# Output projection of a state-space layer divided at half of its 2048 channels, with the decay differences of two head groups on ScalarE

## The chip, the cores and the metric

The kernel runs on one core of one Trainium2 chip. The metric is the device time of one execution in microseconds. A core has five engines that work through instruction streams of their own, each in order: PE (TensorE, with its weight loads shown as PEld), DVE (VectorE), ACT (ScalarE), POOL (GpSimd) and SP (SyncE, which here only issues DMAs). They wait for one another by semaphores.

## The reference

Two layers run over two streams, a prompt of 256 tokens and a sample of 64 with carried state; the kernel treats them as 320 columns side by side. Layer one is a Mamba-2 mixer and a convolutional feed-forward block, layer two is latent attention (MLA) and another such block. Only the Mamba-2 mixer is touched. Cut to what matters:

```
zxbcdt = h @ w_in                                   # 1024 -> 2048 z, 3072 x/B/C, 32 dt
xbc_c  = silu(causal_dwconv(xbc, ...))
dtp    = softplus(dt + dt_bias);  a = -exp(a_log)
# per chunk: acs = cumsum(dtp * a)
seg    = acs[:, :, :, None] - acs[:, :, None]
decay  = exp(where(causal, seg, -inf))
y_diag = einsum(cb * decay * dtp, x);  states, y_off from exp(acs_end - acs), exp(acs)
yg     = rmsnorm over each of 4 groups of 512 channels of (y * silu(z))
out    = yg @ w_out                                 # 2048 -> 1024
```

There are 32 heads of 64 channels in 4 groups of 8 heads; a group is 512 of the 2048 channels.

## The kernel before, in words

**Precision and weights.** Everything is fp32. A product is made of three matmuls (`mm3`, L283 twice and L284 once): high half of the weights by high half of the values, high by low, low by high. Weights come as tiles of 128x1024 fp32 (512 KB) through a ring: SP issues the DMA of a tile into one of 3 buffers `wr`, ACT copies out the high half `wh` (L326), DVE subtracts to get the low half `wl` (L328); there are 4 buffers of each half. Tiles are fetched up to 5 ahead of the one in use (`LD`) and split up to 3 ahead (`LS`).

**Order.** The program is written as a sequence of steps; a scheduler with a simulated timeline then sets the order of the instructions on each engine, by what it reckons is ready. So an edit in one place can move instructions in another. The table `PLAN` sets the sequence in the state-space layer by group g: `conv` (input projection and convolution of x, B, C), `z` (input projection of the gate), `fetch`, `decay`, `scan`, `gate`. The third number says how many pending small steps are let in after each block.

**Decay.** `ssd_fetch` brings, for each of three chunks of 128, 128 and 64 positions, the cumulated log decays of 8 heads, broadcast over the partitions, into a tile `dc` of n x 8 x n elements. `diff` then makes own minus `dc` on DVE (L876, all eight heads in one instruction; L874 first copies out the last column), and clamps it at zero on ACT (L877). `ssd_decay` takes the exponentials on ACT.

**Scan.** `ssd_steps` has 13 small steps per group: `pre` (B and C products, L906 and L907), `xpose` (L918, with `xa` written by DVE L925), `diag` (L935, the products within a chunk, and L943, with the carried state), `states` (L952) and `skip` (L967).

**Gate.** `gate_steps` has three: multiply by silu(z) and square (L982 to L985), sum over the tokens on PE (L362) and the inverse root by Newton steps on DVE (L344 to L350), then `spread` on PE (L369), the multiplication by it on DVE (L992) and the split of each 128-channel block into `ah` (ACT L329) and `al` (DVE L330).

**Output projection.** The 2048 channels are 16 blocks kb of 128 (4 per group), the 1024 outputs 8 blocks m of 128. A product of one block by one output is three matmuls of 320 columns, so the projection has 384. It is divided at channel block 12. The first part takes blocks 0 to 11 (groups 0 to 2) for outputs 0 to 3 and then 4 to 7, in `square_part`: four PSUM tiles `pm` held at once, six weight tiles per half, and after each weight tile `step()` puts in two of the scan and gate steps that are still pending (`LAST` = 2). ACT copies the results into `y` (L771), except that output 7 stays in its PSUM tile. The second part takes blocks 12 to 15 (group 3) for one output after the other; `post` adds the first part (L487, DVE), squares and scales (L497 and L498, ACT) and adds the square to `yacc` (L500, DVE). Before block 15 of output 7, `post_seven` sums `yacc` over the tokens (L362) for the norm that follows.

**Other lines.** L649 and L647 are the convolution, L640 the copy into its input `ext`, L668 the silu, L735 the copy of a gate block out of PSUM, L757 the save of the convolution rows at the end, L644 the POOL copy that feeds it.

Of the kernel before, what the change touches and what calls it, by code (L numbers as in the profile page):

```python
# [17 lines left out]
T = 320  # L18
# [14 lines left out]
DCB = 2  # L33
OUT = 6, 7
SEVEN = 15
# [50 lines left out]
class Kern:  # L86
# [590 lines left out]
    def ssm(self):  # L677
# [3 lines left out]
        with ExitStack() as st:  # L681
# [5 lines left out]
            with ExitStack() as s2:  # L687
# [79 lines left out]
                for half in range(2):  # L767
                    ps = [self.pm() for _ in range(4)]
                    self.square_part(ah, al, range(0, 12, 2), ps, step, 4 - half)
                    for n in range(4 - half):  # L770
                        nc.scalar.activation(out=self.y[:, 4 * half + n, :], in_=ps[n][:, :T], func=AF.Copy)  # L771
                while late:
                    step()
            for half in range(2):
                w = [self.nextw(), self.nextw()]
                for n in range(4):
                    m = 4 * half + n
                    if m > 3:
                        self.early_step(early)
                    p = ps[3] if m == 7 else self.px()  # L780
                    for kb in range(12, 16):
                        if m == 7 and kb == SEVEN:
                            self.post_seven()
                            end = self.pe_end
                        wh, wl = w[kb // 2 - 6]
                        q = slice((kb % 2 * 4 + n) * 128, (kb % 2 * 4 + n) * 128 + 128)
                        last = self.mm3(p[:, :T], wh[:, q], wl[:, q], ah[:, kb, :], al[:, kb, :], kb == 12 and m < 7, kb == 15,
                                        end if m == 7 else None)
                    end = last
                    self.post(p, m, "mix_post0", m < 7)  # L790
# [62 lines left out]
    def ssd_fetch(self, g, sp):  # L853
# [15 lines left out]
        def diff(c):  # L869
            n = CHUNKS[c][1]  # L870
            dc = self.dc[g][c]
            q = 32 * c + 8 * g
            if c:
                nc.vector.tensor_copy(out=self.cd[:, c, 8 * g:8 * g + 8].unsqueeze(2), in_=dc[:, :, n - 1:n])  # L874
            own = self.dtt[:n, 192 + q:200 + q].unsqueeze(2).to_broadcast([n, 8, n])
# [3 lines left out]
        return load, [lambda c=c: diff(c) for c in range(3)]  # L879
# [524 lines left out]
def layout(i):  # L1404
# [16 lines left out]
    wo = f["ssm_w_out"][0].reshape(8, 2, 128, 2, 4, 128).transpose(3, 0, 2, 1, 4, 5).reshape(2, 8, 128, 1024)  # L1421
    out["w_out"] = np.ascontiguousarray(np.concatenate([wo[0, :6], wo[1, :6], wo[0, 6:], wo[1, 6:]], 0))
# [92 lines left out]
```

## Time and profile before

| | |
|---|---|
| median of three timed runs | 995.41 us (995.04 to 996.72) |
| the profiled execution, its own time | 998.17 us |
| its span, first to last instruction | 996.4 us |
| granted TensorE clock over the span | 0.985 |
| 0 to 60 us | PE busy 51.66 us, clock 0.97 |
| 60 to 196.1 us (state-space layer up to the output projection) | PE busy 134.56 of 136.10 us, clock 1.00 |
| 196.1 to 275 us (output projection and its end) | PE busy 75.63 of 78.90 us, clock 0.95 |
| 275 to 996.4 us (the rest of the program) | PE busy 698.07 of 721.40 us, clock 0.99 |

The rows of the trace that follow later give, for a group of instructions, the source line, engine, operation, `out<-in` with the names of the program and shapes, then count, busy time and mean duration; in square brackets stands how long the engine was idle just before and what released it. Rows of a window give its length, then busy time and count for PE, PEld, DVE, ACT and POOL, the granted clock as a share of full speed, the busy share of the DMA engines and GB/s.

### The profile page before, as it was taken

The page shows a single profiled execution, that of the slowest core. Times are in us where ns is not written, and L with a number is a line of the kernel's source. Part 1 is how long each engine was busy: PE and PEld are TensorE (multiplying, and loading weights), DVE is VectorE, ACT ScalarE, POOL GpSimd, SP SyncE. Part 2 cuts the span into 40 slices and gives each one's busy share as a digit, 9 for nine tenths or more (in the row PEclk, how much of TensorE's full clock was granted, in tenths as well). Part 3 has the DMA queues.
Part 4 walks back from the last instruction along what each step waited for, and adds up shares of the span by engine and source line. Part 5 has one row for each costly group of instructions (what it writes and reads, how often), then busy time and mean ns, then how long its engine had stood idle before and what let it go on. Part 6 is the DMA issues. An engine that isn't in the chain of part 4 may idle for free.

```text
span 996.4 us, 18044 instructions
## 1 busy us (share of the span) xinstructions
PE 959.9 (96%) x6585; PEld 929.7 (93%) x6585; DVE 757.7 (76%) x1437; ACT 605.1 (61%) x1201; POOL 350.7 (35%) x597
## 2 busy tenths in 40 slices
PE   7899999999999999999999999999999999999995
PEld 6899999979989999999999899999999999999994
DVE  7879889797488998774547998886538999775433
ACT  6568886734556687664443677774544778665330
POOL 4823231200045665430005765530004767441001
PEclk9999999998999999999999999999999999999998
DMA  7376646442334544455641222133443455445531
GB/s 251 120 212 190 188 138 204 132 154 96 101 94 131 169 149 150 149 186 165 194 125 35 86 70 78 50 102 114 143 136 105 132 167 169 150 143 145 152 115 54
DMA packets 45802, 135.55 MB, mean 136 GB/s; under 512 B 5392, under 2 KB 9616, under 8 KB 45712
## 3 DMA queue, kind: packets, MB, share of 16 engines
q1 hardware_dynamic: 45424, 134.05, 43.1%
q8 instruction: 52, 0.85, 0.4%
q14 instruction: 38, 0.31, 0.1%
q10 hardware_dynamic: 288, 0.33, 0.1%
HBM read 130.25 MB, written 4.11 MB: 135 GB/s over the span
## 4 chain that ended last, share of the span: by engine, by line
PE 79%; DVE 10%; DMA 3%; POOL 3%; issue 3%; ACT 2%; SPq 0%; POOLq 0%; ACTq 0%; DVEq 0%
PE pm L283 46%; PE pm L284 23%; PE px L283 2%; DMA dc<-acd 2%; PE pr L362 1%; PE px L952 1%; DVE wl L328 1%; POOL xacc L442 1%; PE px L284 1%; PE px L943 1%; PE px L935 1%; ACT wh L326 1%; DVE mx L1267 1%; POOL xn L478 1%; DVE y L450 1%
## 5 line engine op out<-in xcount | busy, mean ns | idle before, releaser
L328 DVE TENSOR_TENSOR wl<-wr,wh 128x1024 fp32r<-128x1024 f32 (+2 forms) x204 | 244.8, 1201 | 115.4 <-ACT wh L326 114.6
L326 ACT ACTIVATE wh<-wr 128x1024 fp32r<-128x1024 f32 (+4 forms) x235 | 227.6, 972 | 154.2 <-PE pm L283 126.7
L283 PE MATMUL pm<-xnh,wh 128*128 128x320 f32 x784 | 243.4, 312 | 2.1 <-ACT xnh L329 1.8
L283 PE MATMUL pm<-xnl,wh 128*128 128x320 f32 x784 | 245.0, 313 | 0.3 <-DVE xnl L330 0.3
L284 PE MATMUL pm<-xnh,wl 128*128 128x320 f32 x784 | 243.1, 311 | 0.0
L283 PEld LDWEIGHTS pm<-xnh,wh 128*128 128x128 f32 x784 | 147.6, 189 | 4.8 <-ACT xnh L329 2.0
L283 PEld LDWEIGHTS pm<-xnl,wh 128*128 128x128 f32 x784 | 147.8, 189 | 1.7 <-issue 1.2
L284 PEld LDWEIGHTS pm<-xnh,wl 128*128 128x128 f32 x784 | 147.8, 189 | 1.2 <-issue 1.2
L284 PE MATMUL pm<-ah,wl 128*128 128x320 f32 x452 | 141.0, 313 | 0.0
L283 PE MATMUL pm<-al,wh 128*128 128x320 f32 x452 | 140.4, 311 | 0.0
L283 PE MATMUL pm<-ah,wh 128*128 128x320 f32 x452 | 139.9, 313 | 0.0
L649 DVE SCALAR_TENSOR_TENSOR cv<-ext,vec,cv 128x322 f32<-128x322 f32 x176 | 97.1, 566 | 5.4 <-ACT cv L647 3.0
L643 POOL COPY fsave<-ext 128x2 f32<-128x2 f32 x88 | 72.2, 821 | 53.4 <-ACT ext L640 49.1
L636 POOL MEMSET ext<- 128x2 f32 (+1 forms) x112 | 10.8, 98 | 221.3 <-DVE al L330 66.0
L283 PEld LDWEIGHTS pm<-ah,wh 128*128 128x128 f32 x452 | 85.3, 190 | 1.7 <-ACT ah L329 1.5
L284 PEld LDWEIGHTS pm<-ah,wl 128*128 128x128 f32 x452 | 85.4, 189 | 1.1 <-issue 1.0
L283 PEld LDWEIGHTS pm<-al,wh 128*128 128x128 f32 x452 | 85.5, 189 | 0.0
L328 POOL TENSOR_TENSOR wl<-wr,wh 128x512 fp32r<-128x512 f32 (+2 forms) x31 | 43.7, 1425 | 102.3 <-ACT wh L326 100.9
L283 PE MATMUL pm<-xgl,wh 128*128 128x320 f32 x220 | 68.4, 314 | 1.0 <-DVE xgl L426 1.0
L284 PE MATMUL pm<-xgh,wl 128*128 128x320 f32 x220 | 68.3, 314 | 1.0 <-DVE wl L330 0.7
L283 PE MATMUL pm<-xgh,wh 128*128 128x320 f32 x220 | 62.6, 316 | 4.6 <-ACT xnh L329 2.4
L647 ACT ACTIVATE cv<-ext,vec 128x322 f32<-128x322 f32 x88 | 57.0, 654 | 10.0 <-POOL ext L637 6.8
(396 smaller groups left out, 2138.5 us busy)
## 6 DMA issues: line engine op xcount, KB each, us to landing
wr<-w_up SPq DMA_DIRECT2D x76, 512.0 KB, 3.3
wr<-w_in SPq DMA_DIRECT2D x37, 512.0 KB, 3.8
wr<-w_dn SPq DMA_DIRECT2D x32, 512.0 KB, 3.5
wr<-w_out SPq DMA_DIRECT2D x16, 512.0 KB, 3.6
wr<-w_o SPq DMA_DIRECT2D x16, 512.0 KB, 3.4
wr<-w_up_k SPq DMA_DIRECT2D x16, 384.0 KB, 3.1
wr<-w_dn SPq DMA_DIRECT2D x16, 384.0 KB, 3.2
dc<-acd SPq DMA_DIRECT2D x8, 512.0 KB, 7.0
```

The source lines that it names most:

```text
L283: for i in (mm(out, wh, xh, start=first, stop=False), mm(out, wh, xl, start=False, stop=False), mm(out, wl, xh, start=False, stop=last)):
L284: mm(out, wl, xh, start=False, stop=last)):
L326: self.high_ins = nc.scalar.activation(out=hdst, in_=src, func=AF.Copy).ins
L328: return lambda: e.tensor_tensor(out=ldst, in0=src, in1=hdst.bitcast(F32), op=ALU.subtract)
L362: i = self.nc.tensor.matmul(ps[:, o + b:o + b + 1], acc[:, l0:l0 + 128], self.ones[:, 0:1], start=True, stop=True)
L442: nc.gpsimd.tensor_tensor(out=acc, in0=acc, in1=s, op=ALU.add)
L450: tt(out=yk, in0=yk, in1=r, op=ALU.mult)
L478: nc.gpsimd.tensor_tensor(out=xn, in0=self.x[:, k, :], in1=rstd, op=ALU.mult)
L636: nc.gpsimd.memset(ext[:, 0:m], 0.0)
L643: nc.gpsimd.tensor_copy(out=rows_out[:, 0, :], in_=ext[:, TP:TP + m])
L647: nc.scalar.activation(out=c, in_=ext[:, 0:n], func=AF.Identity, scale=w(0), bias=b)
L649: nc.vector.scalar_tensor_tensor(out=c, in0=ext[:, i:i + n], scalar=w(i), in1=c, op0=ALU.mult, op1=ALU.add)
```

## The change

The projection is divided at channel block 8 in place of 12. The first part now takes groups 0 and 1 only, with four weight tiles per half. The second part takes groups 2 and 3. Its weights are laid out anew on the host, so that one tile of 128x1024 holds blocks 8 to 15 of one output. Outputs 0, 1 and 2 are taken together: group 2's blocks for all three, held in three PSUM tiles `px` with their three weight tiles, then group 3's blocks for all three. Outputs 3 to 7 follow one by one, each with its eight blocks and one weight tile.

For groups 2 and 3 (`WIDE` = 2) `diff` no longer makes one DVE subtraction and one ACT clamp per chunk. ACT does both in one instruction per head: clamp at zero of (−1 · `dc` + own), where own is a column with one value per partition, the bias. It is cut into two pieces of four heads. The copy of the last column stays on DVE. Groups 0 and 1 are as they were.

Lines move by 1 up to the state-space layer's function and by 9 from the scan on (L283 becomes L284, L369 becomes L370, L935 becomes L944); the new ACT instruction is L881.

```
--- before.py
+++ after.py
@@ -31,6 +31,7 @@
         ('z', 3, 3), ('silu', 3, 0), ('gate', 3, 0))
 LAST = 2
 DCB = 2
+WIDE = 2
 OUT = 6, 7
 SEVEN = 15
 LEAD = 2
@@ -766,28 +767,31 @@
 
                 for half in range(2):
                     ps = [self.pm() for _ in range(4)]
-                    self.square_part(ah, al, range(0, 12, 2), ps, step, 4 - half)
+                    self.square_part(ah, al, range(0, 8, 2), ps, step, 4 - half)
                     for n in range(4 - half):
                         nc.scalar.activation(out=self.y[:, 4 * half + n, :], in_=ps[n][:, :T], func=AF.Copy)
                 while late:
                     step()
-            for half in range(2):
-                w = [self.nextw(), self.nextw()]
-                for n in range(4):
-                    m = 4 * half + n
+            for ms in ((0, 1, 2), (3,), (4,), (5,), (6,), (7,)):
+                w, p = {}, {}
+                for m in ms:
                     if m > 3:
                         self.early_step(early)
-                    p = ps[3] if m == 7 else self.px()
-                    for kb in range(12, 16):
-                        if m == 7 and kb == SEVEN:
-                            self.post_seven()
-                            end = self.pe_end
-                        wh, wl = w[kb // 2 - 6]
-                        q = slice((kb % 2 * 4 + n) * 128, (kb % 2 * 4 + n) * 128 + 128)
-                        last = self.mm3(p[:, :T], wh[:, q], wl[:, q], ah[:, kb, :], al[:, kb, :], kb == 12 and m < 7, kb == 15,
-                                        end if m == 7 else None)
-                    end = last
-                    self.post(p, m, "mix_post0", m < 7)
+                    w[m] = self.nextw()
+                    p[m] = ps[3] if m == 7 else self.px()
+                for ks in (range(8, 12), range(12, 16)):
+                    for m in ms:
+                        wh, wl = w[m]
+                        for kb in ks:
+                            if m == 7 and kb == SEVEN:
+                                self.post_seven()
+                                end = self.pe_end
+                            q = slice((kb - 8) * 128, (kb - 8) * 128 + 128)
+                            last = self.mm3(p[m][:, :T], wh[:, q], wl[:, q], ah[:, kb, :], al[:, kb, :], kb == 8 and m < 7, kb == 15,
+                                            end if m == 7 else None)
+                        end = last
+                        if kb == 15:
+                            self.post(p[m], m, "mix_post0", m < 7)
 
     def ssm_conv(self, i, ps, rstd, sp):
         g, i = divmod(i, 10)
@@ -866,17 +870,22 @@
                     for p, r in ((slice(0, 64), r0), (slice(64, 128), r0 + 4)):
                         self.issue(nc.sync.dma_start(out=ea[p].rearrange("p h l -> p (h l)"), in_=src(r, r + 4, 64)))
 
-        def diff(c):
+        def diff(c, hs):
             n = CHUNKS[c][1]
             dc = self.dc[g][c]
-            q = 32 * c + 8 * g
-            if c:
+            q = 192 + 32 * c + 8 * g
+            if c and 0 in hs:
                 nc.vector.tensor_copy(out=self.cd[:, c, 8 * g:8 * g + 8].unsqueeze(2), in_=dc[:, :, n - 1:n])
-            own = self.dtt[:n, 192 + q:200 + q].unsqueeze(2).to_broadcast([n, 8, n])
+            if len(hs) < 8:
+                for h in hs:
+                    nc.scalar.activation(out=dc[:n, h, :], in_=dc[:n, h, :], func=AF.Relu, scale=-1.0, bias=self.dtt[:n, q + h:q + h + 1])
+                return
+            own = self.dtt[:n, q:q + 8].unsqueeze(2).to_broadcast([n, 8, n])
             nc.vector.tensor_tensor(out=dc[:n], in0=own, in1=dc[:n], op=ALU.subtract)
             nc.scalar.activation(out=dc[:n], in_=dc[:n], func=AF.Relu)
 
-        return load, [lambda c=c: diff(c) for c in range(3)]
+        m = 8 if g < WIDE else 4
+        return load, [lambda c=c, h=h: diff(c, range(h, h + m)) for c in range(3) for h in range(0, 8, m)]
 
     def ssd_decay(self, g):
 
@@ -1418,8 +1427,10 @@
             cols += [z[:, g * 512:g * 512 + 512]]
     w = np.concatenate(cols, 1)
     out["w_in_k"], out["w_in"] = _outer(w, 4), _blocks(w[:, 512:])
-    wo = f["ssm_w_out"][0].reshape(8, 2, 128, 2, 4, 128).transpose(3, 0, 2, 1, 4, 5).reshape(2, 8, 128, 1024)
-    out["w_out"] = np.ascontiguousarray(np.concatenate([wo[0, :6], wo[1, :6], wo[0, 6:], wo[1, 6:]], 0))
+    wo = f["ssm_w_out"][0].reshape(2, 1024, 1024)
+    first = wo[0].reshape(4, 2, 128, 2, 4, 128).transpose(3, 0, 2, 1, 4, 5).reshape(8, 128, 1024)
+    rest = wo[1].reshape(8, 128, 8, 128).transpose(2, 1, 0, 3).reshape(8, 128, 1024)
+    out["w_out"] = np.ascontiguousarray(np.concatenate([first, rest], 0))
     out["w_o"] = _square(f["mla_w_o"][0])
     for l in range(2):
         u = f["ffn_w_up"][l].reshape(D, 2, NBF, 128)
```

The scheduler's orders differ between group 1's scan and the end of this projection, and nowhere else. Three places follow; in the names, the numbers behind an underscore tell buffers apart.

**First place: PE, the last scan steps of group 3**, before. L362 and L369 here belong to the gate of group 2.

```order
L362 MATMUL pr_2357<-ones_73,sz_2135 128x1 x3
L935 MATMUL px_2535<-dc_359_2125,xa_2531 64x128 x8
L943 MATMUL px_2544<-ct_1847,hp_2475 128x128 x4
L952 MATMUL px_2551<-xa_2532,bcs_2428 128x512
L918 MATMUL px_2603<-con_71,xs_1911 64x128
L918 MATMUL px_2603<-con_71,xs_1971 64x128
L918 MATMUL px_2603<-con_71,xs_2029 64x128
L918 MATMUL px_2603<-con_71,xs_2089 64x128
L369 MATMUL pr_2373<-con_71,rk_2363 128x128 x3
L935 MATMUL px_2612<-dc_361_2130,xa_2608 64x64 x8
L943 MATMUL px_2621<-ct_1847,h_387_2318 128x64 x4
L952 MATMUL px_2658<-xa_2609,bcs_2490 128x512
```

And in the changed kernel:

```order
L284 MATMUL pm_2608<-ah_101,wh_2611 128x320
L284 MATMUL pm_2608<-al_102,wh_2611 128x320
L285 MATMUL pm_2608<-ah_101,wl_2612 128x320
L944 MATMUL px_2648<-dc_361_2148,xa_2644 64x64 x8
L952 MATMUL px_2657<-ct_1865,h_387_2354 128x64 x4
L961 MATMUL px_2694<-xa_2645,bcs_2526 128x512
L284 MATMUL pm_2804<-ah_101,wh_2666 128x320
L284 MATMUL pm_2804<-al_102,wh_2666 128x320
L285 MATMUL pm_2804<-ah_101,wl_2667 128x320
```

Before, the last two chunks' `diag` and `states` of group 3 stood one behind the other. Now only the last chunk's three lines stand together, with matmuls of the projection's first part (`pm`, values `ah`) ahead of them and behind them.

**Second place: ACT, where the differences of group 2 are made**, before (`dc`, the tile of the decays; `hp`, the carried state; `sz`, the gate):

```order
L326 ACTIVATE wh_1600<-wr_1462 128x1024
L326 ACTIVATE wh_1640<-wr_1520 128x1024
L735 ACTIVATE sz_1597<-pm_1604 128x320
L668 ACTIVATE ct_1306<-ct_1306 128x323
L640 ACTIVATE ext_1494<-pm_1468 128x256
L640 ACTIVATE ext_1494<-pm_1468 128x64
L877 ACTIVATE dc_274_1585<-dc_274_1585 128x1024
L647 ACTIVATE xs_1493<-ext_1494,vec_70 128x323
L955 ACTIVATE hp_1330<-px_1328 128x512
```

And in the changed kernel:

```order
L327 ACTIVATE wh_1600<-wr_1462 128x1024
L881 ACTIVATE dc_274_1585<-dc_274_1585,dtt_613 128x128 x8
L327 ACTIVATE wh_1640<-wr_1520 128x1024
L736 ACTIVATE sz_1597<-pm_1604 128x320
L669 ACTIVATE ct_1306<-ct_1306 128x323
L641 ACTIVATE ext_1494<-pm_1468 128x256
L641 ACTIVATE ext_1494<-pm_1468 128x64
L648 ACTIVATE xs_1493<-ext_1494,vec_70 128x323
L881 ACTIVATE dc_275_1587<-dc_275_1587,dtt_613 128x128 x4
L964 ACTIVATE hp_1330<-px_1328 128x512
L881 ACTIVATE dc_275_1587<-dc_275_1587,dtt_613 128x128 x4
L327 ACTIVATE wh_1676<-wr_1598 128x1024
```

One L877 per chunk is replaced by eight L881, in pieces of four or eight between weight splits (L327) and the instructions of the convolution.

**Third place: PE, the spread of group 3's gate (L369, now L370)**, before, among matmuls of the first part (`pm`):

```order
L283 MATMUL pm_2831<-ah_101,wh_2766 128x320
L283 MATMUL pm_2831<-al_102,wh_2766 128x320
L284 MATMUL pm_2831<-ah_101,wl_2767 128x320
L369 MATMUL pr_2751<-con_71,rk_2711 128x128 x3
L283 MATMUL pm_2829<-ah_101,wh_2796 128x320
L283 MATMUL pm_2829<-al_102,wh_2796 128x320
```

And in the changed kernel, among matmuls of group 2 for the outputs 0 to 2 (`px_2939` is output 0, `px_2946` output 1):

```order
L284 MATMUL px_2946<-ah_101,wh_2870 128x320
L284 MATMUL px_2946<-al_102,wh_2870 128x320
L285 MATMUL px_2946<-ah_101,wl_2871 128x320
L284 MATMUL px_2946<-ah_101,wh_2870 128x320
L370 MATMUL pr_2787<-con_71,rk_2747 128x128 x3
L284 MATMUL px_2946<-al_102,wh_2870 128x320
L285 MATMUL px_2946<-ah_101,wl_2871 128x320
L284 MATMUL px_2946<-ah_101,wh_2870 128x320
```

Before, 91 matmuls of the first part stood between it and the first matmul on group 3's halves. Now it stands behind 19 of the 36 matmuls of group 2 for outputs 0 to 2, and 17 stand between it and the first matmul on group 3's halves.

## The prediction

> **What bounds the kernel now.** I read the share of each engine first, then a table of windows around the output projection, the waits of PE in it, and last the timeline where the table shows a loss.
>
> ```profile
> PE 959.9 (96%) x6585; PEld 929.7 (93%) x6585; DVE 757.7 (76%) x1437; ACT 605.1 (61%) x1201; POOL 350.7 (35%) x597
> ```
>
> PE is the bound, 96% of the span. Moving work between DVE and ACT pays only where PE stands or runs slowly. The next view has per window: length, busy time (and count) of PE, PEld, DVE, ACT, POOL, the granted clock, DMA share and GB/s.
>
> ```profile
> 113.60:140.00 26.40, 26.40 (x194) 24.53 (x193) 25.42 (x45) 18.16 (x33) 11.02 (x16) 1.00 0.54 159
> 150.00:196.10 46.10, 46.10 (x338) 42.85 (x336) 41.06 (x75) 30.70 (x53) 9.89 (x10) 1.00 0.54 170
> 196.10:211.40 15.30, 15.30 (x104) 14.81 (x104) 14.99 (x24) 10.24 (x15) 0.00 (x0) 1.00 0.47 163
> 211.40:229.80 18.40, 16.04 (x110) 12.09 (x109) 18.10 (x41) 3.88 (x8) 0.24 (x2) 0.81 0.32 105
> 255.50:273.00 17.50, 16.59 (x114) 16.10 (x113) 9.20 (x17) 11.65 (x23) 0.00 (x0) 1.00 0.31 91
> ```
>
> The first three are PE without a gap at full clock. From 211.4 to 229.8 PE has gaps, the clock is 0.81, and DVE is busy 18.10 of 18.40 us. PE's waits from 140 to 275 us, all of them:
>
> ```profile
> PE px L935 <- DVE xa L925: 1.2, 1, 1.2
> PE px L935 <- issue: 1.1, 1, 1.1
> PE pr L362 <- ACT ysq L493: 0.5, 1, 0.5
> PE pr L362 <- DVE yacc L500: 0.4, 1, 0.4
> ```
>
> The first two lie in that window, the last two at the end of the projection (near 271 us). The timeline shows why (start, duration):
>
> ```profile
> 216.08 1.09 PE L935 MATMUL px<-dc,xa 128*64 128x128 f32 x16 [1.07 <-issue]
> 221.50 0.68 PE L935 MATMUL px<-dc,xa 64*64 64x64 f32 x16 [1.24 <-DVE xa L925]
> 222.12 1.64 PE L943 MATMUL px<-ct,h 128*128 128x64 f32 x8
> 223.69 2.07 PE L952 MATMUL px<-xa,bcs 64*128 64x512 f32 x2
> 225.69 1.44 PE L283 MATMUL pm<-ah,wh 128*128 128x320 f32 x4
> 227.19 0.47 PE L284 MATMUL pm<-ah,wl 128*128 128x320 f32 x1
> 227.46 0.47 PE L283 MATMUL pm<-al,wh 128*128 128x320 f32 x1
> 230.07 0.31 PE L283 MATMUL pm<-al,wh 128*128 128x320 f32 x1
> 230.22 0.31 PE L284 MATMUL pm<-ah,wl 128*128 128x320 f32 x1
> ```
>
> Two projection matmuls start 0.15 us apart at 230 us, 0.27 us apart at 227 us. Between 211.8 and 225.7 PE has hardly any projection work, because the next block row is group 2, whose halves come from ACT L329. The three rows below are groups 1, 2 and 3; DVE L992 releases group 2 only at 223.47.
>
> ```profile
> 199.67 1.91 ACT L329 ACTIVATE ah<-yg,vec 128x320 fp32r<-128x320 f32 x4
> 223.47 1.92 ACT L329 ACTIVATE ah<-yg,vec 128x320 fp32r<-128x320 f32 x4 [9.59 <-DVE yg L992]
> 244.97 1.93 ACT L329 ACTIVATE ah<-yg,vec 128x320 fp32r<-128x320 f32 x4 [0.94 <-DVE yg L992]
> ```
>
> **The change, part by part.** *Projection split.* The 384 projection matmuls stay 384. What moves is order: the other half of the outputs for groups 0 and 1 (96 matmuls, 14.1 us at 0.147) now stands between the scan steps of group 3, as the first place in the order shows. The window's loss goes with it: the waits, 1.2 + 1.1 = 2.3 us, and the clock, 18.4 x (1 - 0.81) = 3.5 us, together 5.8. A second count: 20 projection matmuls 0.12 slower (2.4), plus two scan steps against the same steps at full clock,
>
> ```profile
> 193.96 1.10 PE L943 MATMUL px<-ct,h 128*128 128x64 f32 x8
> 195.00 1.12 PE L952 MATMUL px<-xa,bcs 64*128 64x512 f32 x2
> ```
>
> 0.54 and 0.95: 3.9, with the waits 6.2. I take **-6.0 us**.
>
> *The last column block.* The wait on yacc (0.4) comes because only 9 matmuls (1.3 us) lie between block 6's end and the sum over tokens. With eight channel blocks in the second part, 21 lie there (3.1 us), and the chain L487, L497, L500 needs about 1.6 us: **-0.4**. The wait on ysq stays.
>
> *Group 3's entry.* This is the new danger. Before, 91 projection matmuls (13.3 us) followed group 3's L369 before group 3 was used. Now 17 do (third place in the order): 2.5 us, with L369's own 0.5 it is 3.0. What has to fit is read from group 3 before:
>
> ```profile
> 237.70 0.72 PE L362 MATMUL pr<-ones,sz 128*128 128x1 f32 x6
> 242.91 0.49 PE L369 MATMUL pr<-con,rk 128*128 128x128 f32 x3
> 243.44 1.49 DVE L992 TENSOR_TENSOR yg<-yg,pr 128x1280 f32<-128x1280 f32 x1 [0.80 <-PE pr L369]
> 245.98 1.93 DVE L330 SCALAR_TENSOR_TENSOR al<-yg,vec,ah 128x320 fp32r<-128x320 f32 x4
> ```
>
> From 242.91 to the first low half (245.98 + 0.55) it is 3.6 us, in which DVE also splits a weight tile (about 1.1). The later low halves come every 0.46 us, and PE takes three matmuls, 0.44, for each. So PE waits between 0 (weight split elsewhere) and 2 us; I take **+0.7**, 3.6 against 3.0 and a little for signals. Three weight pairs are held for outputs 0 to 2 out of four buffers, so output 4's pair can be split only after output 0 is done: its split ends some 10 matmuls before its use, which hides it; if that cover fails it costs about 1.2 us, inside the same bound.
>
> *Differences on ScalarE.* DVE loses six L876 operations, ACT loses six L877 and gains 48 per head (32 of 128x128, 16 of 64x64). Rows (busy, mean ns):
>
> ```profile
> L876 DVE TENSOR_TENSOR dc<-dtt,dc 128x1024 f32<-128x1024 f32 x4 | 4.9, 1226 | 0.0
> L876 DVE TENSOR_TENSOR dc<-dtt,dc 64x512 f32<-64x512 f32 x2 | 1.4, 682 | 0.0
> L877 ACT ACTIVATE dc<-dc 128x1024 f32<-128x1024 f32 x4 | 4.2, 1058 | 1.5 <-DVE dc L876 1.5
> L877 ACT ACTIVATE dc<-dc 64x512 f32<-64x512 f32 x2 | 1.2, 620 | 0.0
> L668 ACT ACTIVATE xs<-xs 128x323 f32<-128x323 f32 x9 | 4.2, 468 | 2.4 <-DVE xs L649 2.2
> L647 ACT ACTIVATE xs<-ext,vec 128x323 f32<-128x323 f32 x8 | 5.0, 652 | 5.5 <-POOL ext L637 4.1 <-DVE yg L967 1.4
> L329 ACT ACTIVATE ah<-yg,vec 128x320 fp32r<-128x320 f32 x5 | 2.5, 550 | 1.8 <-DVE yg L992 1.8
> ```
>
> DVE is relieved of 4.9 + 1.4 = 6.3 us. An ACT operation has a slope of (1058 - 468) / 701 = 0.84 ns per element; one operand per partition adds some 90 ns (550 against 468). So 128 elements with a bias cost an estimated 0.39 us by duration, about 0.30 start to start (the four L329 at 223.47 take 1.92, which is 0.46 apart at 0.55 each), and 64 elements 0.25. Per group ACT gets 16 x 0.30 + 8 x 0.25 = 6.8 us for 2.7. Between 113.6 and 140 us, where group 2's differences are made, ACT is idle 26.40 - 18.16 = 8.2 us, and from 150 to 196, group 3's place, 15 us; that hides the extra 4 us. If it did not, what is late is the weight split and the exponentials queued behind on ACT, then PE. No DMA is added.
>
> *Scan steps moved forward.* The scheduler answers both edits with an earlier order: group 0's L369 now stands 64 block matmuls, some 9 us, earlier on PE.
>
> ```profile
> 145.93 0.16 DVE L350 SCALAR_TENSOR_TENSOR rk<-nwu,rk 128x3 f32<-128x3 f32 x1
> 146.79 0.49 PE L369 MATMUL pr<-con,rk 128*128 128x128 f32 x3
> ```
>
> Before, the last step of the root (L350) ended 0.7 us ahead of L369. DVE's relief until then is half of 6.3, 3.1 us; the remaining 6 us must come from the root's small steps no longer standing between larger ones. With margins like 0.7 us on an in-order PE, each us that DVE or ACT falls behind up to about 160 us is a PE wait. Below nothing is excluded, since PE has no gap there to win; above, the wait is at most the lateness that a per-head chain could add, about 4 us. I take **+1.0**, near the lower end, because PE before met equally narrow margins without a wait.
>
> *SP's queue.* The save of the convolution rows (L757) stood behind the first tile of the output weights and now stands ahead of it and of the last input tile.
>
> ```profile
> SPq L757 <- POOL ssave L644: 9.5, 1, 9.5
> ACT wh L326 <- DMA wr<-w_out: 6.6, 1, 6.6
> ```
>
> It held SP for 9.5 us, and ACT waited 6.6 for the tile behind it, yet PE did not wait: tiles are split three ahead, some 10 us. Its last convolution block now comes earlier on ACT, so I cost the move at nothing; that cover gone, it would cost what exceeds 10 us.
>
> The sum is -6.0 - 0.4 + 0.7 + 1.0 = **-4.7 us**. The profiled execution took 998.17 us (span 996.4 and 1.8 around it), so profiled it would be 993.5. The median of the runs, 995.41, lies 2.8 below; I carry the difference over: 995.41 - 4.7 = **990.7 us**. By the bounds alone (5.8 to 6.2, 0 to 0.4, 0 to 2, 0 to 4) the difference runs from -6.6 to +0.2.
>
> **The rivals.**
>
> *A, the scans stall early.* Group 1's and 2's steps come too early for ACT and DVE and cost the full 4 us: -6.4 + 0.7 + 4 = -1.7, 993.7 us. For it: DVE is busy 25.42 of 26.40 us around 114 to 140. Against: PE stood nowhere from 140 to 211 us.
>
> *B, the wait goes from group 2 to group 3.* DVE is the real bound of the stretch and group 3's values stay at 246.5 us. PE without its loss reaches group 3 near 243: 3.5 us of waiting, and if the clock falls again, up to another 3.5. So -6.4 + 1.0 + 3.5 to 7 = -1.9 to +1.6; I put it at 995. For it: DVE's 18.10 of 18.40. Against: group 3's L362 now stands 84 matmuls, 12.3 us, behind its last scan step, so DVE has time to catch up, and the two groups' differences are gone from DVE before. The Trainium skill, "TensorE: Matmul & The Clock Gate", section "The HAM clock gate (the "warmup" mystery)", says that an idle window of some 3.4 us halves the clock and a busy one of the same length restores it. The trace agrees on the half (0.27 against 0.15), but PE worked from 221.50 to 229.8, 8.3 us, before it was back. By that rule B's second part would be an estimated 1.7 us, by the trace 3.5.
>
> *C, ACT becomes the bound (slower).* If a per-head operation costs what L647 costs, 0.65 us, group 2's 24 take 15.6 us for 2.7: 12.9 more against 8.2 of idle time. ACT is 4.7 us late, the exponentials and weight splits behind it too, PE waits 4.7 and then runs 3.4 us worth of slow clock: -6.4 + 0.7 + 4.7 + 3.4 = +2.4, 997.8 us. It decides from (8.2 + 2.7) / 24 = 0.45 us each. For it: two operands per partition make L647 the dearest of its size. Against: 128 elements are not 323, and there is one such operand. The Trainium skill, "Perfetto Trace Analysis", section "Optimizing Scalar/DVE Operations", speaks against cutting an operation up: each pays about 93 ns of access on ScalarE, and grouping is better where the engine is saturated. By that figure a head would be an estimated 0.20 us, which is below the rows' 0.30.
>
> **How the numbers follow.** Forecast 0.68 (988.5 to 992.8), A 0.13 (992.8 to 994.5), B 0.11 (993.5 to 997), C 0.06, the rest 0.02. A change under 0.2%, 2.0 us, cannot be told from none: 993.4 to 997.4 is "same". Faster gets the forecast, 0.09 of A and 0.04 of B: 0.81. Same gets 0.04 of each: 0.11 with rounding and some of the rest. Slower gets C and what is left: 0.08. The range 988.5 to 994.6 holds the forecast, A and a little of B.
>
> **What would show it.** Right: no gap and clock 1.00 from 196 us to the end of the projection, L362 on yacc without a wait, the projection's end 5 us earlier, and at most a us in front of the first matmul on group 3's halves. L881 near 0.39 us with the rows of L876 gone from DVE for groups 2 and 3. Wrong: PE waits on L943, L935 or L369 between 114 and 160 us (A); a wait of over 3 us on L329 or L330 of group 3 with a clock below 0.9 (B); L881 above 0.45 us and ACT without idle time from 114 to 140 (C); or any difference beyond 275 us, where the order of every engine is unchanged.

## The result and the profile after

The changed kernel took 989.44 us in the median of six runs (987.9 to 990.83), the kernel before 996.72 us beside it (995.04 to 998.56): a ratio of 0.9934, with a 95% interval of 0.9918 to 0.9950, or 5 to 8 us. The forecast was a gain of 4.7 us and a time of 990.7. The profiled execution took 990.83 us with a span of 988.9, against 998.17 and 996.4.

Where the time went is read from three instructions that both kernels have, in the timelines of PE. The first row of each is group 1's second transpose of B (`pre`), ahead of which no engine's order differs; the second is the sum over ysq behind the projection; the third is the next sum over the tokens. Before:

```profile
108.97 0.27 PE L906 MATMUL px<-con,bt 128*128 128x128 f32 x1
272.65 0.83 PE L362 MATMUL pr<-ones,ysq 128*128 128x1 f32 x6 [0.53 <-ACT ysq L493]
302.01 0.72 PE L362 MATMUL pr<-ones,xacc 128*128 128x1 f32 x6
```

After:

```profile
109.54 0.27 PE L915 MATMUL px<-con,bt 128*128 128x128 f32 x1
266.67 0.83 PE L363 MATMUL pr<-ones,ysq 128*128 128x1 f32 x6 [0.53 <-ACT ysq L494]
294.81 0.72 PE L363 MATMUL pr<-ones,xacc 128*128 128x1 f32 x6
```

From the first to the second it is 163.68 us before and 157.13 after, 6.55 less. From the second to the third 29.36 and 28.14, 1.22 less, although no order differs there. Ahead of the first the changed kernel is 0.57 behind, and after the third 0.3 ahead (694.39 against 694.09 to the end of the span). That makes the 7.5 us between the spans. The time from the second to the third is not the same in each execution: the profile of the repeat of the whole change, below, has 26.59 us there in place of 28.14, with a clock of 1.00 where this one falls (0.51 from 292 to 294 us). In what follows the **stretch** is the time from the first to the second of these instructions.

The windows of the changed kernel (the places that the prediction showed of before; length, then busy time and count of PE, PEld, DVE, ACT and POOL, granted clock, DMA share, GB/s):

```profile
113.60:140.00 26.40, 26.40 (x196) 24.49 (x195) 26.40 (x52) 24.18 (x56) 3.52 (x14) 1.00 0.55 162
150.00:196.10 46.10, 46.10 (x340) 43.00 (x339) 40.61 (x75) 35.13 (x76) 4.05 (x10) 1.00 0.53 168
211.40:229.80 18.40, 18.40 (x136) 17.27 (x135) 17.18 (x29) 8.26 (x13) 2.06 (x2) 1.00 0.40 117
```

PE has neither a gap nor a slow clock from 211.4 to 229.8 us. ACT, busy 18.16 us of 26.40 before in the first window, is now at 24.18. PE's waits from 100 to 275 us, all of them:

```profile
PE pr L363 <- ACT ysq L494: 0.5, 1, 0.5
```

And the release of groups 1, 2 and 3 to the projection, in ACT's timeline (ACT writes the high halves `ah` of a group; the low halves follow on DVE):

```profile
186.66 1.91 ACT L330 ACTIVATE ah<-yg,vec 128x320 fp32r<-128x320 f32 x4
216.85 1.93 ACT L330 ACTIVATE ah<-yg,vec 128x320 fp32r<-128x320 f32 x4 [0.45 <-DVE yg L1001]
241.29 1.92 ACT L330 ACTIVATE ah<-yg,vec 128x320 fp32r<-128x320 f32 x4 [3.68 <-DVE yg L1001]
```

Group 2's halves come at 216.85 in place of 223.47, 6.6 us earlier. The instructions per head, grouped by shape (busy, mean ns):

```profile
L881 ACT ACTIVATE dc<-dc,dtt 128x128 f32<-128x128 f32 x32 | 9.9, 396 | 2.1 <-DMA dc<-acd 2.1
L881 ACT ACTIVATE dc<-dc,dtt 64x64 f32<-64x64 f32 x16 | 4.2, 343 | 0.0
```

### The profile page after: what moved, and what is told of

Same layout as the page of the kernel before. It is cut to its first block, busy times and chain, and to the rows that moved or that the text cites. A ratio compares the mean times of both kernels' runs of the same rounds, so it can differ in the third digit from the quotient of the medians.

```text
span 988.9 us, 18082 instructions
## 1 busy us (share of the span) xinstructions
PE 954.9 (97%) x6585; PEld 926.3 (94%) x6585; DVE 752.3 (76%) x1431; ACT 612.2 (62%) x1243; POOL 339.5 (34%) x597
## 4 chain that ended last, share of the span: by engine, by line
PE 77%; DVE 13%; DMA 3%; ACT 3%; issue 2%; POOL 2%; SPq 0%; ACTq 0%; DVEq 0%; POOLq 0%
PE pm L284 44%; PE pm L285 22%; PE px L284 3%; DVE wl L329 2%; DMA dc<-acd 1%; PE px L285 1%; ACT wh L327 1%; PE px L961 1%; PE pr L363 1%; POOL xacc L443 1%; PE px L944 1%; PE px L952 1%; DMA wr<-w_in 1%; DVE mx L1276 1%; DVE xs L650 1%
## 5 line engine op out<-in xcount | busy, mean ns | idle before, releaser
L327 ACT ACTIVATE wh<-wr 128x1024 fp32r<-128x1024 f32 (+4 forms) x235 | 227.6, 972 | 156.1 <-PE pm L284 127.9
L284 PE MATMUL pm<-xnh,wh 128*128 128x320 f32 x784 | 243.8, 312 | 0.7 <-DVE ext L643 0.4
L284 PE MATMUL pm<-xnl,wh 128*128 128x320 f32 x784 | 243.3, 311 | 0.3 <-DVE xnl L331 0.3
L284 PEld LDWEIGHTS pm<-xnh,wh 128*128 128x128 f32 x784 | 146.9, 188 | 3.9 <-issue 2.2
L284 PEld LDWEIGHTS pm<-xnl,wh 128*128 128x128 f32 x784 | 147.1, 188 | 2.5 <-issue 2.0
L284 PE MATMUL pm<-ah,wh 128*128 128x320 f32 x424 | 131.7, 311 | 0.0
L285 PE MATMUL pm<-ah,wl 128*128 128x320 f32 x424 | 131.4, 310 | 0.0
L284 PE MATMUL pm<-al,wh 128*128 128x320 f32 x424 | 131.1, 309 | 0.0
L284 PEld LDWEIGHTS pm<-ah,wh 128*128 128x128 f32 x424 | 79.5, 188 | 1.3 <-ACT y L772 0.8
L284 PEld LDWEIGHTS pm<-al,wh 128*128 128x128 f32 x424 | 79.6, 188 | 0.2 <-issue 0.2
L285 PEld LDWEIGHTS pm<-ah,wl 128*128 128x128 f32 x424 | 79.6, 188 | 0.2 <-issue 0.2
L284 PE MATMUL pm<-xgl,wh 128*128 128x320 f32 x220 | 69.0, 317 | 0.9 <-DVE xgl L427 0.9
L284 PE MATMUL pm<-xgh,wh 128*128 128x320 f32 x220 | 63.2, 319 | 4.7 <-DVE v L822 2.4
```

The source lines that it names most:

```text
L284: for i in (mm(out, wh, xh, start=first, stop=False), mm(out, wh, xl, start=False, stop=False), mm(out, wl, xh, start=False, stop=last)):
L285: mm(out, wl, xh, start=False, stop=last)):
L327: self.high_ins = nc.scalar.activation(out=hdst, in_=src, func=AF.Copy).ins
```

## The experiments

Two theories stood at the start. **S**, the prediction's: the division at half carries the gain, because projection matmuls then stand among group 3's scan steps. **D**: the differences carry it. With them off DVE the scheduler sets the scans and gates earlier, so that group 2 is ready in time for the projection whichever way it is divided. The order of the instructions spoke for D: with the differences alone, the scan and gate steps up to group 3's scan stand at the same places as in the whole change, and with the division alone they stand where they stood before, up to the first chunk of group 3's scan. Each ratio is against runs of the kernel before on the same chip in the same series.

**The division alone.**

```
-WIDE = 2
+WIDE = 4
```

> The projection split at half, with the differences of all four groups on DVE as before (WIDE = 4). Theory S (the prediction: the split carries the gain): PE has no gap among group 3's scan steps and at most 2 us in front of group 3's first projection matmul; 4 to 7 us faster than before. Theory D (the differences carry it): the scheduler leaves the scans where they were, and in this order group 3's sum over the tokens (L363) and its spread (L370) stand one directly behind the other and directly in front of the first matmul on group 3's halves. PE then waits there for the Newton root, about 1.9 us, and for the multiplication and the first halves, about 3 us, and the clock may fall for up to 3.5 us more: of a gain of 6.4 in the earlier window some 5 to 8 us are given back; 2 us faster to 2 us slower than before.

Measured: 994.35 us against 995.22, ratio 0.9990 (0.9977 to 1.0003): no difference that can be told. The stretch took 163.38 us, 0.3 less than before. PE's waits from 110 to 275 us, and two windows:

```profile
PE px L284 <- ACT ah L330: 2.2, 1, 2.2
PE pr L370 <- DVE rk L351: 1.6, 1, 1.6
PE pr L363 <- ACT ysq L494: 0.5, 1, 0.5
```

```profile
215.00:235.00 20.00, 20.00 (x154) 18.03 (x153) 18.27 (x37) 6.78 (x11) 2.26 (x2) 1.00 0.38 132
235.00:250.00 15.00, 11.23 (x63) 10.93 (x62) 7.12 (x16) 3.58 (x6) 0.39 (x4) 0.77 0.11 36
```

The loss among the scan steps is gone, as S says; it has moved to **group 3's entry**, the place where PE first needs group 3's halves, as D says. PE waits 1.6 us for the root and 2.2 for the first halves, and the clock falls there. Group 2 is as late as before:

```profile
222.92 1.92 ACT L330 ACTIVATE ah<-yg,vec 128x320 fp32r<-128x320 f32 x4 [4.67 <-DVE yg L1001]
244.01 1.92 ACT L330 ACTIVATE ah<-yg,vec 128x320 fp32r<-128x320 f32 x4 [7.35 <-DVE yg L1001]
```

Dividing earlier lets PE do other work while group 2 is late, but this work is then missing while group 3 is late.

**The differences alone.** The kernel before with only this part of the change:

```
+        m = 8 if g < WIDE else 4
+        return load, [lambda c=c, h=h: diff(c, range(h, h + m)) for c in range(3) for h in range(0, 8, m)]
```

> The projection divided at block 12 as before, and only the differences of groups 2 and 3 on ScalarE. Theory S: the loss among group 3's scan steps (two waits of 1.2 and 1.1 us, clock 0.81) stays, so the time is that of before, or up to 1 us more. Theory D: group 2's spread now stands 37 projection matmuls, 5.4 us, ahead of the first matmul on group 2's halves, where it stood at none before; the entry takes about 3.6 us, so the loss goes without the split: 5.5 to 7 us faster than before. What stays is the wait on yacc at the end, 0.4 us, and a clock below 1.00 for some us behind it, 1.3 us; so 1 to 2 us slower than the whole change.

Measured: 990.06 us, ratio 0.9950 (0.9931 to 0.9968). The stretch took 157.39 us, 6.3 less than before and 0.3 more than with the whole change. Group 2's release, and PE's waits from 110 to 275 us:

```profile
215.98 1.92 ACT L330 ACTIVATE ah<-yg,vec 128x320 fp32r<-128x320 f32 x4 [0.44 <-DVE yg L998]
```

```profile
PE pr L363 <- ACT ysq L494: 0.5, 1, 0.5
PE pr L363 <- DVE yacc L501: 0.4, 1, 0.4
```

S is refuted: without the division the loss among the scan steps is gone all the same. What remains beside the whole change is the wait on yacc and a clock of 0.50 behind it, looked at below.

**The whole change again**, in the same series:

> The whole change again, beside the others on the same chip: 6 to 8 us faster than before by either theory.

Measured: 987.65 us, ratio 0.9925 (0.9904 to 0.9946), stretch 157.12 us. By the medians of this series the division is worth 0.9 us without the differences, which cannot be told from nothing, and 2.4 us with them; the differences are worth 5.2 us without the division.

**One group at a time.** D leaves open what about the differences counts: DVE's time as such (D1, each us alike) or one place that was too late (D2). Both runs keep the division at block 12.

```
-        m = 8 if g < WIDE else 4
+        m = 4 if g == 2 else 8
```

> The projection divided at block 12 as before; the differences of group 2 alone on ScalarE, so DVE is relieved of 3.1 us in place of 6.3. Theory D1 (each us of DVE relief counts alike): half the gain of both groups, 2.5 to 3.5 us faster than before. Theory D2 (there is one place where group 2's gate was too late, and any relief that brings its spread ahead of the projection's use by about 3.6 us takes the loss away): group 2's spread stands 19 projection matmuls, 2.8 us, ahead of the first matmul on group 2's halves, so PE stands 0.8 us at most: 4.5 to 6 us faster.

And with `g == 3`:

> As the run before, with the differences of group 3 alone on ScalarE. Theory D1: 2.5 to 3.5 us faster than before. Theory D2: group 2's spread stands 17 projection matmuls, 2.5 us, ahead of its use; PE stands 1.1 us at most: 4 to 6 us faster. If only relief early in the stretch (group 2's differences, 113 to 140 us) counts: no gain.

Measured: group 2 alone 989.85 us against 996.50, ratio 0.9933 (0.9913 to 0.9953), stretch 158.6; group 3 alone 991.64 us, ratio 0.9950 (0.9933 to 0.9966), stretch 158.4. Either relief, half as large, takes nearly the whole loss away (5.1 and 5.3 us of the stretch), so D1 is refuted. Group 2's release and the one wait left there, with group 2 alone:

```profile
215.78 1.92 ACT L330 ACTIVATE ah<-yg,vec 128x320 fp32r<-128x320 f32 x4 [5.27 <-DVE yg L998]
217.98 0.68 PE L941 MATMUL px<-dc,xa 64*64 64x64 f32 x16 [0.59 <-DVE xa L931]
```

With group 3 alone:

```profile
218.71 1.90 ACT L330 ACTIVATE ah<-yg,vec 128x320 fp32r<-128x320 f32 x4
218.83 0.68 PE L941 MATMUL px<-dc,xa 64*64 64x64 f32 x16 [0.97 <-DVE xa L931]
```

The wait is not where D2 put it, at group 2's entry, but at the last scan step of group 3, where 1.24 us stood before. Group 3's differences are made long after group 2's, so it is not the early part of the stretch that has to be relieved.

**Another piece of DVE work.**

```
-                 (xpose, 2), (diag, 2), (states, 2), (skip, 0))
+                 (xpose, 2), (diag, 2), (states, 2)) + (() if g in (1, 2) else ((skip, 0),))
```

> The kernel before, with all differences on DVE and the projection divided at block 12; left out is another piece of DVE work near the same places, the skip term of groups 1 and 2 (y + x D, eight DVE instructions of each group, about 2.5 us a group by the rows of L976), so this part of the result is missing. Theory D2 says that DVE's time ahead of group 2's gate is what counts, and not the differences or ScalarE: group 2's spread then stands 33 projection matmuls, 4.9 us, ahead of its use, and the kernel is 5 to 7 us faster than before, like the differences alone. If the gain came from the differences being ready earlier or in pieces: within 1.5 us of before.

Measured: 989.54 us, ratio 0.9932 (0.9916 to 0.9947), stretch 157.8, with no wait from 109 to 262 us. Group 2's release:

```profile
210.45 1.92 ACT L329 ACTIVATE ah<-yg,vec 128x320 fp32r<-128x320 f32 x4 [3.13 <-DVE yg L992]
```

So neither ScalarE nor the differences are what counts, but DVE's time ahead of group 2's gate and group 3's last scan step. These are three ways of freeing 3 to 6 us of DVE there, and each brings about the same. This run alone would not show it, since group 2's skip term also stands in the chain of group 2's own gate; but group 3's differences do not, and their relief brings group 2 in time as well. How early group 2 comes is not the gain: here its halves come 11.3 us earlier than before, counted from the start of the stretch, and the stretch is 5.8 us shorter. It is enough that they are in time.

What is not separated is DVE's freed time from the order that the scheduler made of it. In each of the four faster versions with the division at block 12, group 2's spread stands 17 to 37 projection matmuls ahead of the first matmul on group 2's halves, where it stood at none before. No run has the new order without the relief, or the relief in the old order.

**ScalarE's bound.** Rival C, with the pieces cut in two:

```
+                    for o in range(0, n, n // 2):
+                        nc.scalar.activation(out=dc[:n, h, o:o + n // 2], in_=dc[:n, h, o:o + n // 2], func=AF.Relu, scale=-1.0,
```

> The whole change with each difference on ScalarE cut into two halves (96 instructions for the two groups in place of 48): ScalarE pays about 12 us a group, estimated from 0.396 us for 128 columns and 0.343 for 64, in place of 7. The idle time of ScalarE from 113.6 to 140 us was 2.2 us in the whole change. Rival C's bound: ScalarE is some 3 us late for group 2, and in this order group 3's spread stands directly in front of the first matmul on group 3's halves, about 3 us too late: 3 to 7 us slower than the whole change, near or above the time before. If ScalarE's idle time elsewhere takes it: within 1 us of the whole change.

Measured: 992.60 us against 996.50, ratio 0.9962 (0.9944 to 0.9979), stretch 162.5 us, 5.4 longer than with the whole change. Part of it is ScalarE's queue, part again group 3's entry: waits of 1.3 and 2.2 us, and a clock of 0.95, 0.50 and 0.70 in the three windows of 2 us from 243 to 249 us, which costs another 1.7. The shapes, the window in which group 2's differences are made, and PE's waits from 109 to 275 us:

```profile
L882 ACT ACTIVATE dc<-dc,dtt 128x64 f32<-128x64 f32 x64 | 16.8, 346 | 0.0
L882 ACT ACTIVATE dc<-dc,dtt 64x32 f32<-64x32 f32 x32 | 7.6, 334 | 0.0
```

```profile
113.60:140.00 26.40, 25.06 (x185) 22.89 (x184) 24.12 (x46) 26.07 (x78) 5.24 (x16) 1.00 0.39 134
```

```profile
PE px L284 <- ACT ah L330: 2.2, 1, 2.2
PE pm L284 <- ACT sz L736: 1.3, 1, 1.3
PE pr L363 <- ACT ysq L494: 0.5, 1, 0.5
```

ScalarE is full from 113.6 to 140 (26.07 of 26.40), and PE waits 1.3 us for a PSUM tile that ACT (L736) has not copied out. The whole change, at 24.18, is 2.2 us from this bound.

**More groups on ScalarE.** `WIDE = 1` and `WIDE = 0`, with the division at half:

> The whole change with the differences of group 1 on ScalarE too (WIDE = 1). Between 60 and 113.6 us ScalarE is busy about 43 us of 53.6 and VectorE about 45; group 1's pieces add about 4 us to ScalarE and take 3 from VectorE. There PE still waits 1.2 to 3 us, on yg L946 of ScalarE and on cd L878 and dc L921 of VectorE. If VectorE is what is late there: up to 2 us faster than the whole change. If ScalarE's queue is (yg L946): 0.5 to 3 us slower than it. From 113.6 us on as the whole change.

> The whole change with the differences of all four groups on ScalarE (WIDE = 0). Group 0's are made between 40 and 60 us, where PE waits for other things. The same two cases as for three groups, with 8 us more on ScalarE ahead of 113.6 us: up to 2 us faster than the whole change if VectorE is late there, 1 to 5 us slower if ScalarE is.

Measured: 991.80 and 993.05 us against 996.36, ratios 0.9965 (0.9950 to 0.9981) and 0.9975 (0.9962 to 0.9989): 3 to 5 us above the whole change's ratio. PE waits for ScalarE (three groups, then four, 109 to 275 us):

```profile
PE pm L284 <- ACT ext L641: 1.1, 1, 1.1
```

```profile
PE pm L284 <- ACT sz L736: 0.8, 1, 0.8
PE pm L284 <- ACT ext L641: 0.6, 1, 0.6
```

This is nearer the second case of the expectation, that more relief for DVE is paid on ScalarE, but not at the instruction named there: the wait on yg L946 is 0.5 and 1.0 us, against 1.1 in the whole change. The two waits on ext stand at 112.2 and 111.5 us, the wait on sz with four groups at 122.1 us. Together they are 1.1 and 1.4 us, less than the 3 to 5 us by the ratios; where the rest is lost was not found.

**Group 3's entry.** The division at half, with group 2 alone on ScalarE:

> The projection divided at half, as in the whole change, but with the differences of group 2 alone on ScalarE; divided at block 12 the same pair was as fast as the whole change. In this order group 3's spread stands directly in front of the first matmul on group 3's halves, where it stands 17 matmuls ahead in the whole change and 91 with the division at block 12. If group 3's entry is what the division at half puts at risk: PE stands 2 to 2.5 us there and the clock falls for 1 to 3.5 us; 3 to 6 us slower than the whole change, 1 to 4 us faster than before. If the division at half costs nothing there, the time of the whole change.

Measured: 991.01 us against 996.36, ratio 0.9955 (0.9942 to 0.9968), 2 to 3 us above the whole change's and so below the 3 to 6 expected; stretch 160.95 us, 3.8 longer than with the whole change. PE's timeline at the entry (the spread L370, the first matmuls on group 3's halves, and two later ones):

```profile
240.04 0.49 PE L370 MATMUL pr<-con,rk 128*128 128x128 f32 x3
242.70 1.17 PE L284 MATMUL px<-ah,wh 128*128 128x320 f32 x3 [2.17 <-ACT ah L330]
243.66 0.47 PE L284 MATMUL px<-al,wh 128*128 128x320 f32 x1
243.93 0.47 PE L285 MATMUL px<-ah,wl 128*128 128x320 f32 x1
```

From the spread to the first high half it is 2.66 us. With nothing between them PE stands 2.2, and the clock falls to half (matmuls 0.27 us apart): 1.6 of the 3.8 us. In the whole change 17 matmuls, 2.5 us, lie there.

**The wait on yacc and the clock behind it.** In the whole change the clock stays at 1.00 for some 20 us behind the projection; before, it fell there (0.78, 0.50 and 0.87 in the three windows of 2 us behind the sum over ysq). Two runs ask whether the wait of 0.4 us on yacc does that. The first puts the sum earlier (`SEVEN = 11`):

> The whole change, but the sum over the tokens of yacc stands 12 matmuls earlier in the last output (SEVEN = 11), so that 9 matmuls lie between output 6's end and it, as before the change. If the wait on yacc and the slower clock behind the projection are one thing: a wait of about 0.4 us on yacc comes back, the clock in the 10 us behind it falls below 0.9, and the kernel is 1 to 2 us slower than the whole change. If the clock there has another cause (the earlier loss near 211 to 230 us): only the wait of 0.4 us.

Measured: 988.60 us, ratio 0.9932 (0.9914 to 0.9950), against 0.9925 for the whole change in the same series. The wait on yacc, 0.4 us, was back, and the clock behind it was 1.00: the second case. But this moved the two sums apart, 3.6 us in place of 1.9. The second run leaves them together:

```
-            for ms in ((0, 1, 2), (3,), (4,), (5,), (6,), (7,)):
+            for ms in ((0, 1, 2), (3,), (4,), (5,), (6, 7)):
```

> The whole change, but outputs 6 and 7 are taken together in the second part: group 2's blocks for both, then group 3's for output 6, then for output 7. So 9 matmuls lie between output 6's end and the sum over yacc, and the sum over ysq follows 1.9 us behind it, as before the change; everything up to there is as in the whole change. Theory E (a wait on yacc of 0.4 us and the wait on ysq of 0.5 us within 2 us lower the clock): the wait of 0.4 comes back, the clock in the four us behind the sum over ysq is about 0.5 to 0.8, and the kernel is 1.5 to 4 us slower than the whole change. If the clock there has another cause: the wait of 0.4 us comes back and nothing else, within 1 us of the whole change.

Measured: 990.18 us against 996.17, ratio 0.9947 (0.9931 to 0.9963), 1.3 to 2.2 us above the whole change's ratios, 0.9934 and 0.9925, though the intervals overlap. The profiled execution shows the wait and no slow clock:

```profile
PE pr L363 <- ACT ysq L494: 0.5, 1, 0.5
PE pr L363 <- DVE yacc L501: 0.4, 1, 0.4
```

The profiled run had 988.49 us and a mean clock of 0.992; the other five had 0.988 to 0.990 and 989.39 to 992.48 us. Of the whole change, all six runs of the repeat had 0.992, but the first six had 0.988 to 0.992, so the mean clock does not tell the two apart. Over all profiles, the clock fell behind the sum over ysq in four of the six that have both waits within 2 us (before, the differences alone, and each group alone), and in none of the others. This agrees with theory E without settling it, since no run of the last kernel with a lower clock was profiled. By the profiles of the differences alone and of the repeat, the division's worth beside the differences, 2.4 us, would be 0.3 of stretch and 2.1 behind it (28.65 against 26.59); but the first profile of the whole change has 28.14 there, so how much of the 2.1 belongs to the division stays open.

No version here beat the whole change by more than the runs can tell.

## Why the prediction was right, and where it was not

The time was in the range, 1.3 us below the number forecast. That it came so near is partly luck: the gain was 7.3 us against 4.7, and the kernel before had a median of 996.72 us beside it, in place of the 995.41 that the forecast was counted from. The account behind it was right about what was lost before and wrong about what takes the loss away.

- **What bounds.** Right: the 5.8 to 6.2 us among group 3's scan steps were the loss, and group 2's late halves its cause. The stretch became 6.55 us shorter, against 6.4 with the wait on yacc.
- **"Projection split. ... The window's loss goes with it", -6.0.** This step failed. The division alone gains nothing that can be told; the differences alone give 6.3 us of the stretch. It took the mixing of projection matmuls and scan steps in the changed order for an effect of the division, when the scheduler sets the same scan places with the differences alone.
- **"Scan steps moved forward", +1.0.** Wrong in sign. It was priced as a danger, "each us that DVE or ACT falls behind ... is a PE wait". PE waited nowhere from 109 us to the end of the projection, and the earlier steps are the gain: group 2's halves come 6.6 us earlier. DVE's relief had been counted, 6.3 us, but had no term in the sum and was not followed to the instruction that was late.
- **Group 3's entry, +0.7 (0 to 2).** It measured 0 in the whole change. The prediction had PE take three matmuls, 0.44 us, for each low half. In the whole change three products of a high half stand first. The second block's high half is ready only near 242.30 us (241.29 + 0.46 + 0.55), so these three must be one block for the three outputs, which gives the low half time. The rows, of PE and of DVE:

```profile
242.07 0.60 PE L284 MATMUL px<-ah,wh 128*128 128x320 f32 x3
242.51 0.41 PE L284 MATMUL px<-al,wh 128*128 128x320 f32 x1
```

```profile
241.89 1.94 DVE L331 SCALAR_TENSOR_TENSOR al<-yg,vec,ah 128x320 fp32r<-128x320 f32 x4 [0.63 <-ACT ah L330]
```

  The first low half is ready near 242.44 (241.89 + 0.55) and is used at 242.51. The danger was real: in three experiments PE stood 2.2 us there.
- **Differences on ScalarE.** 0.396 us for 128 columns (estimate 0.39) and 0.343 for 64 (0.25). Start to start, 0.29 and 0.24 (rows of eight take 2.45 and 2.01 us), so 6.6 us a group against 6.8. The idle time hid it.
- **The last column block, -0.4.** The wait went. The 1.22 us more behind the projection were not foreseen; they are the clock behind the sum over ysq, which fell there before and did not in the whole change.
- **SP's queue, 0.** Right; PE met no wait from it. The save's wait on SP was 9.5 us before and is now 3.0:

```profile
SPq L758 <- POOL ssave L645: 3.0, 1, 3.0
```

- **Rivals.** A did not come. C exists: at about half a us a head (two halves of 0.24 each) ScalarE was full. Its place is as told, but PE's wait on ACT was 1.3 us there, with 2.2 us more and a slow clock worth 1.7 at group 3's entry. B, "the wait goes from group 2 to group 3", is what the division alone does.

The sum's errors, -6.0 credited to the wrong half and +1.7 of dangers that did not come, did not show in the time. With only the division made, the same working would have promised 5.7 us that were not there.

## What to carry to other kernels

Where an engine in order waits because a value is late, ask which engine makes it late, and credit the gain to the edit that relieves that engine; an edit that gives the waiting engine other work only moves the wait to the next late value. Where a scheduler sets the order, look at the order of each part of a change alone before dividing a gain among the parts. Relief of a nearly full engine need not pay evenly: half of it here brought nearly all, and twice of it made the kernel slower again.

## What the runs showed of the hardware

The slow clock comes in pieces. Before, in windows of 2 us from 221 to 231 us, the granted clock was:

```profile
221.00:223.00 2.00, 1.50 (x22) 1.43 (x22) 2.00 (x3) 0.00 (x0) 0.00 (x0) 0.88 0.35 131
223.00:225.00 2.00, 2.00 (x6) 1.07 (x5) 2.00 (x6) 1.52 (x4) 0.00 (x0) 0.50 0.03 8
225.00:227.00 2.00, 2.00 (x6) 1.31 (x6) 2.00 (x6) 0.39 (x1) 0.00 (x0) 0.50 0.00 0
227.00:229.00 2.00, 2.00 (x9) 2.00 (x8) 2.00 (x6) 0.00 (x0) 0.24 (x2) 0.50 0.01 4
229.00:231.00 2.00, 2.00 (x14) 2.00 (x14) 1.97 (x4) 0.00 (x0) 0.00 (x0) 0.92 0.35 131
```

At half speed this is (0.12 + 0.50 + 0.50 + 0.50 + 0.08) x 2 / 0.5 = 6.8 us of slow clock. With group 2 alone and the division at half it is one piece of half that length:

```profile
242.00:244.00 2.00, 1.30 (x5) 1.30 (x6) 1.37 (x4) 1.91 (x4) 0.00 (x0) 0.67 0.00 0
244.00:246.00 2.00, 2.00 (x9) 2.00 (x8) 0.62 (x2) 0.01 (x1) 0.39 (x4) 0.50 0.00 0
246.00:248.00 2.00, 2.00 (x16) 2.00 (x15) 0.00 (x0) 0.00 (x0) 0.00 (x0) 0.98 0.00 0
```

(0.33 + 0.50 + 0.02) x 4 = 3.4 us. So a fall costs 1.7 or 3.4 us where PE has work throughout. The Trainium skill, "TensorE: Matmul & The Clock Gate", section "The HAM clock gate (the "warmup" mystery)", has the clock set by the activity in a free-running window of about 3.4 us; the lengths here are one and two of it. The prediction held 8.3 us against that rule, counted from PE's first instruction behind the gap and not from the fall of the clock; the rule's half on the return to full speed agrees with these lengths, and its 1.7 us with the 1.6 above. The other half, an idle window of that length before the fall, does not fit: a gap of 2.2 us was enough, and behind the waits of 0.4 and 0.5 us within 2 us the clock fell in four profiles of six. Nor does it fall alike in each execution: the 28 runs of the kernel before in one series have mean clocks from 0.985 to 0.994, and the profile of before, from which the loss was read, has 0.985.

The instruction per head on ScalarE (clamp with a bias per partition, fp32) has a fixed part of 0.185 us from start to start, by the rows of two runs: two halves of 64 columns take 2 x 0.239 (21 in 5.12 us), one of 128 takes 0.293 (eight in 2.45), and the difference is the fixed part.
